# Eight raw weight buffers instead of four in a fused decoder layer with a streamed mixture of experts, and a new order of a few norm, gather and sum steps

## The chip, the cores and the metric

One core of one Trainium2 chip runs the kernel as one launch. The metric is the device time of an execution in microseconds (us), median over runs; lower is better. All data is float32 in HBM. TensorE (PE in the rows) does the matmuls, VectorE is DVE, ScalarE is ACT, GpSimd is POOL, and SP is the queue engine from which nearly all loads are issued, one after the other.

## The reference

One layer over T = 256 tokens of width 1024, batch 1:

```
n  = rmsnorm(x) ;  proj = n @ w_in                  # 1024 x 5136
o_a = gated linear attention(4 heads) ; o_b = differential attention(4 heads)
merged = sigmoid(gate_a) * (o_a @ w_branch_a) + sigmoid(gate_b) * (o_b @ w_branch_b)
h  = x + merged @ w_out
n2 = rmsnorm(h) ;  group = argmax of 4 ; top 2 of the 8 experts in the group
h += sum over 32 experts of comb[e] * ((silu(n2 @ w_gate[e]) * (n2 @ w_up[e])) @ w_down[e])   # 1024 x 256 x 1024 each
h += sigmoid(h @ w_ple_gate) * rmsnorm(p @ w_ple)
out = rmsnorm(h)
```

The expert weights alone are 96 MB, and all of them are read whichever experts the tokens choose.

## The kernel before, in words

**Dense part.** The dense weights are cut into 114 pieces, called units: 8 of `gqk`, 2 of `w_al`, 8 each of `gv`, `dq`, `dk`, `dv` and `gr`, 32 of the gates `sg`, 16 of the branch matrices `y` and 16 of `w_out` (`wo`). A piece is 128x512 float32, 256 KB (the two of `w_al` are smaller). For each piece `raw_load` (L341) takes a buffer with the tag `w_raw` (4 of them) and issues its load on SP; `part` (L347) splits it into a high half, which ACT copies, and a low half, which DVE subtracts (`gv_h` and `gv_l` in the rows, made from `gv_r`); then six matmuls of 512 columns use the two halves: for each of the two token tiles high by high, low by high and high by low. `run` (L383) walks the units in order: it has the loads issued up to unit i+5 and the splitting up to unit i+3. The mixer's own chains (attention, norms, gates) are generators that advance between units.

**Expert weights.** 100 tiles of 1 MB hold the experts' weights and the gate `w_ple_gate`: 8 gate or up tiles and 4 down tiles for each quartet of experts q0 to q7 (`NQ` is 8), and `w_ple_gate` between the down tiles of the last two quartets. They rotate through 23 slots (`ring`, L200); slots 11 to 21 are free from the start, the others hold tensors of the dense part until these die. `NFREE` says how many tiles may be loaded from the start. Every third unit `run` issues one half tile (`refill(whole=False)`) on SP between the raw loads. After the last unit `refill(2 + len(fill))` issues the rest that fits, whole tiles: 23 tiles lie in SBUF before an expert has run, and each later one waits on SP until the matmuls have read the tile that had its slot. SP works in order: a load that waits holds up all that stand behind it.

**Transition.** The last three `w_out` units are held and run by token tile (`out_unit`, L850). `h1_half` (DVE) adds the residual into `xh`; `h1_turn` transposes `xh` on PE (`ph1T`) and copies it out (`h1T`, on ACT, the last on DVE); `h1_square` (ACT) squares `xh` and writes the squares to the spent PSUM bank of `w_out`, which for token tile 0 is the bank that the router's sums `pr` take next. `logits` are the router matmuls `pr`. `inv_root` makes the norm's factor `rstd2`: a DVE addition and a power on POOL with the exponent `mhalf`. `route(t)` is the chain for the top group and the top 2 on DVE, with a small PE matmul `pk` for ranks. `gather(0, t)` multiplies by a one-hot matrix (`pq`) to collect the tokens of the first quartet (`pxg` on PE, evicted into `xg` by DVE); for token tile 0 it yields after its first steps until `pk` of token tile 1 has been issued.

**Experts and end.** `experts_in(q)` runs gate and up (`ph`), then down (`py`), per quartet. In the last quartet the down sums come in quarters (`pyq`, evicted into `ys_last`) and are scattered back to token order by `pz`. Four DVE adds put the output of quartets 0 to 6 and `xh` into `hn`, one 128x512 piece each; `hn` lies in the slot of an expert tile that has been read. Then `pz` is added into `hn`, `hn` is transposed (`ph2T`, copied out as `h2T`), and the gate matmuls `pg` run quarter by quarter. A list of steps (L1383) orders the last gate and norm: `sig`, `mul`, `add`, `square`, `normed` (`sgs = hn * rows`, on POOL or, where V is given, on DVE), `root` (`inv_root` into `ro`), `scaled`, `finished`.

Of the kernel before, what the change touches and what calls it, by code (L numbers as in the profile page):

```python
# [32 lines left out]
NSLOT = 22  # L33
NFREE = NSLOT - 11
ROWS = 8
# [28 lines left out]
def kernel(  # L64
# [38 lines left out]
    def col(t, a):  # L103
        return a[:, t:t + 1]
# [94 lines left out]

    ring = list(range(11, NSLOT)) + [2, 5, 3, 6, 8, 7, 4, 9, 10, 1, 0, NSLOT]  # L200
    ring2 = ring[:15] + ring[19:-1]
# [136 lines left out]
    back, side = lanes = [[], []]  # L338

    def raw_load(i):  # L340
        if i < len(units) and i not in raws and i not in parts and i >= state["i"]:  # L341
            src, kc, n, name = units[i][0]
            raws[i] = wst.tile([P, kc, n], F32, tag="w_raw", name=f"{name}_r", bufs=4)
            Y.dma_start(raws[i], src.rearrange("(k p) n -> p k n", p=P))

    def part(i):
        if i < len(units) and i not in parts:  # L347
            src, kc, n, name = units[i][0]
            if i == 0:
                x_parts(0, [0])  # L350
            elif i < KC:
                x_parts(i)
            if units[i][3]:
                parts[i] = [wst.tile([P, kc, n], F32R, tag=f"w_{c}", name=f"{name}_{c}") for c in "hl"]
                split(parts[i][0], parts[i][1], raws.pop(i), None)
            else:
                parts[i] = raws.pop(i)
            if i == 0:
                x_parts(0, [1])
# [23 lines left out]
    def run(upto):  # L383
        while state["i"] < upto:
            i = state["i"]
            for a in range(5):
                raw_load(i + a)
                if a < 3:
                    part(i + a)
            units[i][1](parts.pop(i))  # L390
            state["i"] = i + 1
            part(i + 3)
            raw_load(i + 5)
            if units[i][2]:
# [428 lines left out]
    for n in range(2):  # L823
        for b, w in enumerate((w_branch_a, w_branch_b)):
            stream([oTs[b][:, i] for i in range(2)], 4, w, n * 512, f"y{b}{n}", branch(b, n), (acc_bank, bank)[n * b])
    accw, held = [], []

    ss2 = cst.tile([P, NT, 2], F32, name="ss2")
# [18 lines left out]
    def h1_square(t, n):  # L847
        A.activation(accw[t][n], xh[:, t, n * 512:(n + 1) * 512], AF.Square, scale=1.0 / 32, accum_out=ss2[:, t, n:n + 1])

    def out_mm(t, n, k, ws):  # L850
        mm3(accw[t][n], [a[:, k, t * P:(t + 1) * P] for a in mT], [w_[:, 0, :] for w_ in ws], k == 0, k == KC - 1)

    def out_unit(k, n):
        def f(ws):
# [17 lines left out]
            h1_half(1, 0)  # L872
            out_mm(1, 1, 6, w61)
            for n_ in range(2):
                h1_turn(0, n_)
            out_mm(1, 1, 7, w71)
            h1_half(1, 1)
            for n_ in range(2):
                h1_square(0, n_)
        return f  # L880

    for k in range(KC):
        for n in range(2):
            units.append(((w_out[k * P:(k + 1) * P, n * 512:(n + 1) * 512], 1, 512, f"wo{n}_{k}"), out_unit(k, n),
                          (lambda: fill.extend(range(2))) if (k, n) == (1, 1) else None, True))

    state["quiet"] = len(units) - 8
    run(len(units))
    while back:
        step()  # L890
    refill(2 + len(fill))
    del fill[:]
# [7 lines left out]
    logits(0, 0)  # L900
    for n in range(2):
        h1_turn(1, n)
    logits(0, 1)
    h1_square(1, 0)
    h1_square(1, 1)
    logits(1, 0)
    logits(1, 1)
# [41 lines left out]
    rk = wk.tile([P, NT, NE], F32, name="rk")  # L949
    rstd2 = wk.tile([P, NT], F32, name="rstd2")  # L950
    mhalf = wk.tile([P, 1], F32, name="mhalf")
    Q.memset(mhalf, -0.5)

    def inv_root(y, ms):

        V.scalar_tensor_tensor(y, ms[0], EPS, ms[1], ALU.add, ALU.add)
        Q.tensor_tensor(y, y, mhalf, ALU.pow)

    for t in range(NT):
        inv_root(col(t, rstd2), (ss2[:, t, 0:1], ss2[:, t, 1:2]))  # L960

# [30 lines left out]
    def route(t):  # L992
# [20 lines left out]
        for i, _ in enumerate(gather(0, t)):  # L1013
            if i:
                yield from until("pk1")
# [124 lines left out]
    def experts_in(q):  # L1140
# [30 lines left out]
        for h in range(2):  # L1171
            last = q == NQ - 1 and h == 1
            E.on = E.on or last
            wts = [wtiles.pop(("gu", q, 4 * h + j)) for j in range(4)]
# [67 lines left out]
    for c in range(LATE):  # L1242
# [3 lines left out]
        wsl[q] = wk.tile([P, 1], F32, name=f"wsl{q}")  # L1246
    last_ys = []

# [18 lines left out]


    first = tiles.index(("gu", NQ - 1, 6))
    hn = slot(slot_of(first - 4), [NT, D], F32, "hn")  # L1270
    for t in range(NT):
        for n in range(2):
            cs = slice(n * 512, (n + 1) * 512)
            V.tensor_tensor(by_rows(hn[:, t, cs]), by_rows(yp[t][n]), by_runs(t, n), ALU.add)
    V.on = A.on = E.on = Q.on = True
# [107 lines left out]
    for f, *a in ((sig, b00), (mul, b00), (sig, b01), (add, b00), (mul, b01), (sig, b10), (square, b00), (normed, 0, 0, 512), (add, b01),  # L1383
                  (mul, b10), (sig, h0), (sig, h1), (normed, 0, 512, 1024), (square, b01), (add, b10), (mul, h0), (square, b10),
                  (add, h0), (root, 0), (mul, h1), (scaled, 0, 0, 512), (square, h0), (add, h1), (scaled, 0, 512, 1024), (square_v, h1),
                  (root, 1), (normed, 1, 0, 512, V), (finished, 1, 512, 768), (scaled, 1, 0, 512, A), (finished, 1, 768, 1024)):
        f(*a)
# [31 lines left out]
```

## Time and profile before

| | |
|---|---|
| median of 3 runs | 448.23 us (448.19 to 448.48) |
| profiled execution | 448.06 us, of which its span is 446.5 us |
| PE busy, DVE busy | 407.3 us (91%), 218.3 us (49%) |
| ACT busy, POOL busy | 154.5 us (35%), 35.7 us (8%) |
| HBM read | 137.62 MB, 311 GB/s over the span |
| mean granted clock of PE | 0.965 |

The profile's page gives whole-span shares; the stages have different limits, so the stretches are read apart: 0 to 201 us the dense units, 201 to 217 us the transition, 217 to 387 us the expert stream, 387 to 436 us the last quartet and the gate, 436 to 446.5 us the last norm. "<-" in brackets names what ended an engine's idle time and how long that was. PE's busy time contains modelled ends of pipelined matmuls, so starts of matmuls are the safer thing to read.

### The profile page before, as it was taken

How to read it: one execution, taken by the hardware profiler on the slowest of the kernel's cores; microseconds unless marked ns; L12 is line 12 of the kernel's file. 1: busy time of each engine (PE TensorE's matmuls, PEld its weight loads, DVE VectorE, ACT ScalarE, POOL GpSimd, SP SyncE). 2: the span in 40 equal slices, each digit the busy share in tenths (PEclk: the TensorE clock that was granted, in tenths of full speed). 3: DMA queues.
4: the chain of work that ended last, by engine and by line, in shares of the span. 5: the costliest groups of instructions: out<-in, count | busy, mean ns of one | idle time of the engine just before them, and what ended most of it. 6: DMA issues, size and time to landing. Idle time of an engine off the chain costs nothing. (4 is left out here: it accounts for less than half of the span.)

```text
span 446.5 us, 7553 instructions
## 1 busy us (share of the span) xinstructions
PE 407.3 (91%) x2876; PEld 273.0 (61%) x2876; DVE 218.3 (49%) x478; ACT 154.5 (35%) x335; POOL 35.7 (8%) x83
## 2 busy tenths in 40 slices
PE   7999999999998999988898988899997998869990
PEld 4767777778786877868545545445263266436670
DVE  4657765896978468656403121222141163073545
ACT  5748645588555535436000000000010100042334
POOL 7200004000160000001000000000000000000003
PEclk9999999999999999999989999989899799988996
DMA  7688875678878888889599999999999999999502
GB/s 222 175 265 277 286 241 156 226 244 283 289 226 275 278 302 274 287 333 349 188 426 418 420 415 420 418 421 419 418 420 420 423 419 420 382 370 364 206 0 94
DMA packets 47214, 139.18 MB, mean 312 GB/s; under 512 B 7282, under 2 KB 17222, under 8 KB 38088
## 3 DMA queue, kind: packets, MB, share of 16 engines
q1 hardware_dynamic: 46872, 138.35, 84.5%
q8 instruction: 23, 0.38, 0.4%
q10 hardware_dynamic: 144, 0.26, 0.2%
q14 instruction: 15, 0.12, 0.1%
q0 software_dynamic: 160, 0.07, 0.1%
HBM read 137.62 MB, written 1.05 MB: 311 GB/s over the span
## 5 line engine op out<-in xcount | busy, mean ns | idle before, releaser
L58 PE MATMUL ph<-wt,xg 128*32 128x256 f32 x1024 | 61.4, 380 | 1.4 <-DMA wt<-in_w_up_dram 1.4
L58 PEld LDWEIGHTS ph<-wt,xg 128*32 128x32 f32 x1024 | 34.4, 110 | 24.5 <-DMA wt<-in_w_up_dram 1.8
L58 ACT ACTIVATE misc<-ph 128x256 f32<-128x256 f32 x8 | 3.1, 384 | 114.6 <-PE ph L58 114.6
L58 PE MATMUL sg<-sg_h,xT 128*128 128x512 f32 x128 | 40.3, 396 | 0.0
L58 PE MATMUL py<-wt,misc 128*32 128x512 f32 x192 | 32.6, 714 | 6.7 <-DVE misc L58 4.7
L58 PEld LDWEIGHTS pxg<-pq,xh 128*128 128x128 f32 x256 | 29.6, 192 | 5.2 <-issue 2.7
L58 PE MATMUL pxg<-pq,xh 128*128 128x128 f32 x256 | 30.4, 276 | 1.9 <-PEq L1061 1.6
L58 DVE TENSOR_TENSOR sg_l<-sg_r,sg_h 128x512 fp32r<-128x512 f32 x32 | 23.5, 736 | 10.5 <-ACT sg_h L58 10.4
L58 PE MATMUL pg<-wg,h2T 128*128 128x512 f32 x96 | 27.2, 420 | 0.7 <-ACT h2T L58 0.7
L58 PEld LDWEIGHTS sg<-sg_h,xT 128*128 128x128 f32 x128 | 23.4, 188 | 4.3
L58 PE MATMUL sg<-sg_l,xT 128*128 128x512 f32 x64 | 25.3, 395 | 0.1
L58 ACT ACTIVATE sg_h<-sg_r 128x512 fp32r<-128x512 f32 x32 | 19.9, 628 | 14.6 <-DMA sg_r<-in_w_in_dram 8.9
L58 PEld LDWEIGHTS py<-wt,misc 128*32 128x32 f32 x192 | 7.4, 124 | 26.8 <-issue 16.0
L58 DVE TENSOR_TENSOR xg<-pxg,g_exp 128x512 f32<-128x512 f32 x16 | 11.0, 690 | 23.0 <-PE pxg L58 22.7
L58 DVE SCALAR_TENSOR_TENSOR misc<-df,wr 128x128 f32<-128x128 bf16 x16 | 3.9, 288 | 37.1 <-PE phT L58 37.0
L58 PEld LDWEIGHTS pg<-wg,h2T 128*128 128x128 f32 x96 | 17.5, 198 | 7.2 <-issue 2.9
L58 PE MATMUL wo<-wo_h,mT 128*128 128x512 f32 x64 | 20.2, 396 | 1.3 <-ACT wo_h L58 1.3
L58 POOL TENSOR_TENSOR sgs<-hn,rows 128x512 f32<-128x512 f32 x2 | 2.5, 1282 | 229.3 <-DVE hn L58 229.3
L58 PE MATMUL y<-y_h,oT 128*128 128x512 f32 x64 | 20.1, 395 | 0.0
L58 DVE TENSOR_TENSOR wo_l<-wo_r,wo_h 128x512 fp32r<-128x512 f32 x16 | 11.0, 691 | 10.2 <-ACT wo_h L58 9.8
L58 DVE TENSOR_TENSOR y_l<-y_r,y_h 128x512 fp32r<-128x512 f32 x16 | 10.9, 691 | 8.3 <-ACT y_h L58 8.3
L58 PE MATMUL y<-late,misc 128*128 128x512 f32 x32 | 14.9, 608 | 0.0
(312 smaller groups left out, 738.7 us busy)
## 6 DMA issues: line engine op xcount, KB each, us to landing
wt<-in_w_up_dram SPq DMA_DIRECT2D x27, 1024.0 KB, 19.2
wt<-in_w_gate_dram SPq DMA_DIRECT2D x24, 1024.0 KB, 19.8
wt<-in_w_down_dram SPq DMA_DIRECT2D x20, 1024.0 KB, 19.8
wt<-in_w_down_dram SPq DMA_DIRECT2D x24, 512.0 KB, 9.3
wt<-in_w_gate_dram SPq DMA_DIRECT2D x16, 512.0 KB, 5.2
sg_r<-in_w_in_dram SPq DMA_DIRECT2D x32, 256.0 KB, 3.2
wt<-in_w_up_dram SPq DMA_DIRECT2D x10, 512.0 KB, 4.5
wo_r<-in_w_out_dram SPq DMA_DIRECT2D x16, 256.0 KB, 4.7
```

What stands on the lines that cost most here:

```text
L58: ins = getattr(self.engine, name)(*args, **kwargs)
```

## The change

1. Raw weight pieces have eight buffers: four with the tag `w_raw`, four in `more`, which is slot 20 of the experts' slots; groups of four units alternate. Loads are issued up to unit i+8 instead of i+5. The two halves of the very last unit go into two `w_raw` buffers.
2. `NFREE` is 10 instead of 11 and `ring` is reordered: slot 20 gets its first tile only at the transition, where three whole tiles more than `len(fill)` are issued instead of two. During the units 16 tiles are loaded instead of 17.
3. `h1_square(0, 0)` is issued ahead of the two transposes of token tile 0. `rstd2` and its exponent lie in the dead tiles `sinT` and `cosT`, and `rstd2` of a token tile is computed as soon as its squares are, between the transposes.
4. Token tile 0's gather goes on to its third step before it waits for `pk` of token tile 1.
5. The four adds into `hn` are issued (`own_order`) ahead of the last half of the last quartet's gate and up matmuls.
6. In the final list `normed(1, 0, 512)` moves from DVE to POOL and up, `root 0` ahead of `add h0`, and `scaled 0` behind `add h1`.

```diff
-NFREE = NSLOT - 11
+NFREE = NSLOT - 12
...
-    ring = list(range(11, NSLOT)) + [2, 5, 3, 6, 8, 7, 4, 9, 10, 1, 0, NSLOT]
+    ring = list(range(11, NSLOT - 2)) + [NSLOT - 1, 2, 5, 3, 6, 8, 7, 4, 9, 10, NSLOT - 2, 1, 0, NSLOT]
...
+    more = slot(NSLOT - 2, [4, 512], F32, "more_r")
...
-            raws[i] = wst.tile([P, kc, n], F32, tag="w_raw", name=f"{name}_r", bufs=4)
+
+            raws[i] = wst.tile([P, kc, n], F32, tag="w_raw", name=f"{name}_r", bufs=4) if (i + 2) // 4 % 2 else \
+                more[:, (i + 2) % 4, :].rearrange("p (k n) -> p k n", k=kc)
...
-                parts[i] = [wst.tile([P, kc, n], F32R, tag=f"w_{c}", name=f"{name}_{c}") for c in "hl"]
+                tag, bufs = ("w_raw",) * 2 if i == state.get("last") else ("w_h", "w_l"), 4 if i == state.get("last") else None
+                parts[i] = [wst.tile([P, kc, n], F32R, tag=tag[c], name=f"{name}_{'hl'[c]}", bufs=bufs) for c in range(2)]
...
-            for a in range(5):
+            for a in range(8):
...
-            raw_load(i + 5)
+            raw_load(i + 8)
...
+    rstd2, mhalf = sinT[:, 0, 0:2], cosT[:, 0, 0:1]
+    Q.memset(mhalf, -0.5)
...
+            h1_square(0, 0)
             for n_ in range(2):
                 h1_turn(0, n_)
             out_mm(1, 1, 7, w71)
             h1_half(1, 1)
-            for n_ in range(2):
-                h1_square(0, n_)
+            h1_square(0, 1)
...
-    refill(2 + len(fill))
+    refill(3 + len(fill))
...
     logits(0, 0)
-    for n in range(2):
-        h1_turn(1, n)
+    h1_turn(1, 0)
+    norm2(0)
+    h1_turn(1, 1)
     logits(0, 1)
     h1_square(1, 0)
     h1_square(1, 1)
+    norm2(1)
...
-            if i:
+            if i > 2:
                 yield from until("pk1")
...
+            if last:
+                own_order()
...
+    def own_order():
+
+        hn_.append(slot(slot_of(first - 4), [NT, D], F32, "hn"))
+        for t in range(NT):
+            for n in range(2):
+                cs = slice(n * 512, (n + 1) * 512)
+                V.tensor_tensor(by_rows(hn_[0][:, t, cs]), by_rows(yp[t][n]), by_runs(t, n), ALU.add)
...
-                  (add, h0), (root, 0), (mul, h1), (scaled, 0, 0, 512), (square, h0), (add, h1), (scaled, 0, 512, 1024), (square_v, h1),
-                  (root, 1), (normed, 1, 0, 512, V), (finished, 1, 512, 768), (scaled, 1, 0, 512, A), (finished, 1, 768, 1024)):
+                  (normed, 1, 0, 512), (root, 0), (add, h0), (mul, h1), (square, h0), (add, h1), (scaled, 0, 0, 512), (square_v, h1),
+                  (root, 1), (scaled, 0, 512, 1024), (finished, 1, 512, 768), (scaled, 1, 0, 512, A), (finished, 1, 768, 1024)):
```

The first place is SP around the last raw loads of `w_out`; `wo_5_r` is the raw piece of `w_out`'s row block 5, `wt` an expert tile (128x2048 is a whole one, 128x1024 a half), and the two fences are the kernel before and the changed one.

```order
L58 DMA wo_4_r<-in_w_out_dram 128x512
L58 DMA wo_5_r<-in_w_out_dram 128x512 x2
L58 DMA wt_2054<-in_w_up_dram 128x1024
L58 DMA wo_6_r<-in_w_out_dram 128x512 x2
L58 DMA wo_7_r<-in_w_out_dram 128x512 x2
L58 DMA wt_2054<-in_w_up_dram 128x1024
L58 DMA wt_2162<-in_w_up_dram 128x2048
```

```order
L58 DMA wo_4_r<-in_w_out_dram 128x512 x2
L58 DMA wo_5_r<-in_w_out_dram 128x512 x2
L58 DMA wt_1962<-in_w_gate_dram 128x1024
L58 DMA more_r<-in_w_out_dram 128x512 x3
L58 DMA wt_1962<-in_w_gate_dram 128x1024
L58 DMA more_r<-in_w_out_dram 128x512
L58 DMA wt_2104<-in_w_up_dram 128x2048
```

The last four raw pieces are loaded into `more`, and they are issued up to eight units ahead of their matmuls instead of five; behind the last of them no half tile is left, and whole tiles follow at once.

The second place is ACT in the transition, where `wo_0` and `wo_1` are the spent `w_out` banks that take the squares of token tiles 0 and 1, and `h1T` the copies of the transposes.

```order
L58 ACTIVATE wo_7_h<-wo_7_r 128x512 x2
L58 ACTIVATE h1T_2147<-ph1T_2142 128x512
L58 ACTIVATE h1T_2154<-ph1T_2149 128x512
L58 ACTIVATE wo_0_1947,ss_1659<-xh 128x512
L58 ACTIVATE wo_0_1948,ss_1659<-xh 128x512
L58 ACTIVATE h1T_2184<-ph1T_2179 128x512
```

```order
L58 ACTIVATE wo_7_h<-more_r 128x512 x2
L58 ACTIVATE wo_0_1901,ss_1619<-xh 128x512
L58 ACTIVATE h1T_2090<-ph1T_2085 128x512
L58 ACTIVATE h1T_2097<-ph1T_2092 128x512
L58 ACTIVATE wo_0_1902,ss_1619<-xh 128x512
L58 ACTIVATE h1T_2127<-ph1T_2122 128x512
```

One square has moved from behind the two copies to ahead of them; the other stays behind.

The third place is DVE in the last quartet: `misc` is the quartet's gated product, `ys_last` the evicted down sums, `hn` the sum that the last gate reads.

```order
L58 CAST oT_last<-pws_3540 128x256
L58 SCALAR_TENSOR_TENSOR misc<-misc,wsl_3378,ph_3548 128x256
L58 TENSOR_TENSOR ys_last<-pyq_3622,ys_last 128x256
L58 COPY misc<-phT_3619 128x256
L58 TENSOR_TENSOR hn<-y_2435,xh 128x512
L58 TENSOR_TENSOR hn<-y_2436,xh 128x512
L58 TENSOR_TENSOR hn<-y_2437,xh 128x512
L58 TENSOR_TENSOR hn<-y_2438,xh 128x512
L58 TENSOR_TENSOR ys_last<-pyq_3650,ys_last 128x256
```

```order
L58 CAST oT_last<-pws_3480 128x256
L58 TENSOR_TENSOR hn<-y_2375,xh 128x512
L58 TENSOR_TENSOR hn<-y_2376,xh 128x512
L58 TENSOR_TENSOR hn<-y_2377,xh 128x512
L58 TENSOR_TENSOR hn<-y_2378,xh 128x512
L58 SCALAR_TENSOR_TENSOR misc<-misc,wsl_3318,ph_3488 128x256
L58 TENSOR_TENSOR ys_last<-pyq_3567,ys_last 128x256
L58 COPY misc<-phT_3564 128x256
L58 TENSOR_TENSOR ys_last<-pyq_3590,ys_last 128x256
```

The four adds stand ahead of the gated product instead of between the two evictions of the down sums.

## Rows read from the trace of the kernel before

**Rows 1.** A piece of the chain of waits: start, length, what.

```profile
367.12 19.95 DMA wt<-in_w_up_dram
```

**Rows 2.** SP's issues at the transition, by the timeline; the fourth of them waits for the first slot that the experts free.

```profile
200.89 16.40 SPq L58 DMA_DIRECT2D wt<-in_w_down_dram  x4
```

**Rows 3.** Windows: the stretch and its length, then busy time and count of PE, PEld, DVE, ACT and POOL, then granted clock of PE, DMA share, GB/s.

```profile
211.50:217.00 5.50, 5.50 (x88) 3.92 (x90) 3.18 (x10) 0.43 (x1) 0.00 (x0) 1.00 0.08 31
220.00:387.00 167.00, 150.51 (x1406) 79.94 (x1398) 41.00 (x105) 9.03 (x21) 0.00 (x0) 0.95 1.01 419
398.30:405.00 6.70, 5.83 (x26) 3.23 (x27) 3.50 (x5) 0.98 (x2) 0.00 (x0) 0.51 1.07 372
405.00:420.00 15.00, 15.00 (x108) 10.46 (x108) 5.90 (x9) 5.54 (x8) 0.00 (x0) 0.99 1.00 343
```

**Rows 4.** Timeline of SP (issues) and PE while the `gv` units run: start, length, engine, operation, and the idle time before it with what ended it.

```profile
15.86 5.96 SPq L58 DMA_DIRECT2D gv_r<-in_w_in_dram  x4
25.68 0.73 PE L58 MATMUL gv<-gv_h,xT 128*128 128x512 f32 x2 [0.44 <-ACT gv_h L58]
33.71 0.73 PE L58 MATMUL gv<-gv_h,xT 128*128 128x512 f32 x2 [0.59 <-ACT gv_h L58]
34.69 0.50 PE L58 MATMUL gv<-gv_l,xT 128*128 128x512 f32 x1 [0.24 <-DVE gv_l L58]
```

**Rows 5.** One row of PE's waits over the first 200 us: who waited for whom, us in total, times, longest.

```profile
PE poT L58 <- DVE osl L58: 1.6, 2, 0.8
```

**Rows 6.** Timeline of SP, ACT and PE at the end of `w_out`, columns as in rows 4.

```profile
186.46 3.81 SPq L58 DMA_DIRECT2D wo_r<-in_w_out_dram  x4
195.96 0.63 ACT L58 ACTIVATE wo_h<-wo_r 128x512 fp32r<-128x512 f32 x1 [2.56 <-DMA wo_r<-in_w_out_dram]
194.52 0.62 PE L58 MATMUL wo<-wo_h,mT 128*128 128x512 f32 x2
194.98 0.40 PE L58 MATMUL wo<-wo_l,mT 128*128 128x512 f32 x1
196.64 0.73 PE L58 MATMUL wo<-wo_h,mT 128*128 128x512 f32 x2 [1.26 <-ACT wo_h L58]
199.31 1.09 PE L58 MATMUL ph1T<-ident,xh 128*128 128x128 f32 x8
200.16 0.70 PE L58 MATMUL wo<-wo_h,mT 128*128 128x512 f32 x2
200.70 0.40 PE L58 MATMUL wo<-wo_l,mT 128*128 128x512 f32 x1
```

**Rows 7.** Timeline of ACT and PE at the first router sums.

```profile
200.97 0.61 ACT L58 ACTIVATE wo<-xh 128x512 f32<-128x512 f32 x1
201.80 1.05 PE L58 MATMUL pr<-wr,h1T 128*128 128x40 f32 x8 [0.70 <-issue]
```

**Rows 8.** Timeline of PE in the gather for the first quartet.

```profile
209.96 0.18 PE L58 MATMUL pk<-Mb,scr 128*128 128x32 bf16 x1 [0.32 <-DVE Mb L58]
209.99 3.37 PE L58 MATMUL pxg<-pq,xh 128*128 128x128 f32 x28
```

**Rows 9.** Timeline of ACT, DVE and PE after the last expert tile has landed.

```profile
394.24 0.38 ACT L58 ACTIVATE ys_last<-pyq 128x256 fp32r<-128x256 f32 x1 [0.69 <-PE pyq L58]
392.74 3.95 DVE L58 TENSOR_TENSOR hn<-y,xh 128x512 f32<-128x512 f32 x4
396.60 0.42 DVE L58 TENSOR_TENSOR ys_last<-pyq,ys_last 128x256 fp32r<-128x256 f32 x1
397.08 0.62 PE L58 MATMUL pz<-ys_last,oT_last 128*128 128x256 f32 x3 [2.02 <-DVE ys_last L58]
398.48 1.12 PE L58 MATMUL ph2T<-ident,hn 128*128 128x128 f32 x4 [0.79 <-DVE hn L58]
400.28 1.65 PE L58 MATMUL pg<-wg,h2T 128*128 128x512 f32 x3 [0.69 <-ACT h2T L58]
401.86 1.94 PE L58 MATMUL pyq<-wt,misc 128*32 128x256 f32 x16
406.70 1.07 PE L58 MATMUL pyq<-wt,misc 128*32 128x256 f32 x16
410.60 0.60 PE L58 MATMUL ph2T<-ident,hn 128*128 128x128 f32 x4
412.78 1.07 PE L58 MATMUL pyq<-wt,misc 128*32 128x256 f32 x16
416.08 1.07 PE L58 MATMUL pyq<-wt,misc 128*32 128x256 f32 x16
```

**Rows 10.** Timeline of DVE and POOL at two places where both work in SBUF: the first two rows in the dense part, the others at the end.

```profile
135.44 0.69 DVE L58 TENSOR_TENSOR rs_a<-ro 128x8 f32<-128x8 f32 x1
135.28 0.83 POOL L58 TENSOR_TENSOR wr<-wr,g_exp 128x320 f32<-128x320 f32 x1 [4.97 <-DMA wr<-in_w_router_expert_dram]
435.40 2.55 POOL L58 TENSOR_TENSOR sgs<-hn,rows 128x512 f32<-128x512 f32 x2 [229.34 <-DVE hn L58]
438.87 0.55 POOL L58 TENSOR_TENSOR ro<-ro,mhalf 128x1 f32<-128x1 f32 x1 [0.93 <-DVE ro L58]
440.88 0.69 DVE L58 TENSOR_TENSOR sgs<-hn,rows 128x512 f32<-128x512 f32 x1
441.04 0.93 POOL L58 TENSOR_TENSOR ro<-ro,mhalf 128x1 f32<-128x1 f32 x1 [1.62 <-DVE ro L58]
```

More of the change, by code (lines that the diff above doesn't have):

```diff
@@ L826, with inv_root, norm2 @@
     accw, held = [], []
+    rstd2, mhalf = sinT[:, 0, 0:2], cosT[:, 0, 0:1]
+    Q.memset(mhalf, -0.5)
+    def inv_root(y, ms):
+        V.scalar_tensor_tensor(y, ms[0], EPS, ms[1], ALU.add, ALU.add)
+        Q.tensor_tensor(y, y, mhalf, ALU.pow)
+    def norm2(t):
+        inv_root(col(t, rstd2), (ss2[:, t, 0:1], ss2[:, t, 1:2]))
     ss2 = cst.tile([P, NT, 2], F32, name="ss2")
@@ L885 @@
                           (lambda: fill.extend(range(2))) if (k, n) == (1, 1) else None, True))
+    state["last"] = len(units) - 1
     state["quiet"] = len(units) - 8
@@ L949 @@
     rk = wk.tile([P, NT, NE], F32, name="rk")
[L950 to L960, printed above, removed]
     def sm(shape, name, dt=F32):
@@ L1246 @@
         wsl[q] = wk.tile([P, 1], F32, name=f"wsl{q}")
-    last_ys = []
+    last_ys, hn_ = [], []
+    first = tiles.index(("gu", NQ - 1, 6))
+    def own_order():
[4 more added lines that the diff above has]
+                V.tensor_tensor(by_rows(hn_[0][:, t, cs]), by_rows(yp[t][n]), by_runs(t, n), ALU.add)
     def outs_of(c, i):
@@ L1265 @@
         experts_in(q)
[L1269 to L1274, printed above, removed]
+    hn = hn_[0]
     V.on = A.on = E.on = Q.on = True
```

## The prediction, made before the changed kernel ran

> **What bounds the kernel now.** I read the chain of waits first, then windows by stage, then the timelines at the seams. The chain's piece that ends last before the tail is the load of an expert tile, 367.12 + 19.95 = 387.07 [rows 1]. The windows say why: from 220 to 387 the DMA share is 1.01 at 419 GB/s, while PE has 16 us of the 167 to spare [rows 3]. So there the time is bytes over rate, and nothing that engines gain inside the stretch shortens it. What counts is when the stream may start. SP's fourth issue in the group that begins at 200.89 goes out at the group's end, 200.89 + 16.40 less its own third of a microsecond, at 217.0: a tile has to wait for the first slot that an expert's matmuls free [rows 2]. Ahead of it the DMA engines stand nearly idle, share 0.08 from 211.5 to 217 [rows 3], since the 23 tiles that fit are already in. The kernel therefore falls into three parts in series: PE work and chains of latencies up to the first freed slot; a stream of fixed length, 387.1 - 217.0 = 170 us; a tail of PE, DVE and ACT behind the last tile. A microsecond taken from the first or the third comes off the total; one taken from the second by an engine does not.
>
> **The change part by part.** *A tile's load moved from the units into the transition.* 23 tiles are in before the first slot comes free in both kernels; only 16 instead of 17 of them load during the units. The tile moved costs 1 MB at 419 GB/s, 2.5 us of DMA, against 5.5 us in which DMA idles at 0.08 [rows 3]. I cost it at nothing; if that cover were gone it would be at most 2.5.
>
> *Eight buffers, early.* While `gv` runs, SP takes 5.96 us to issue four raw loads, which wait for buffers [rows 4]. Each wait becomes a late piece: PE stands 0.44 + 0.59 + 0.24 = 1.27 us for `gv` halves [rows 4]. With loads issued eight units ahead the pieces are in when they are wanted; I take 1.3. PE's other waits of these 200 us are for the mixers' own chains, the largest 1.6 us for `osl` [rows 5]; they hang on DVE, not on loads, and might go if DVE is held less by late halves. Bounds: 0.5 if only one `gv` wait goes, 2.9 if the 1.6 goes too.
>
> *Eight buffers, end of `w_out`.* The four last raw loads take SP 3.81 us from 186.46, the last issue thus at about 190.0; its piece ends ACT's wait of 2.56 at 195.96, and PE stands 1.26 from there [rows 6]. Worked on PE's clock of starts: two columns-of-512 matmuls are 194.98 - 194.52 = 0.46 apart, 0.23 each, so PE is free at 195.21. From there come 12 more such matmuls (2.76) and the 8 transposes (200.16 - 199.31 = 0.85): 198.8 without waits. Before, the last one ends its turn at 200.70 + 0.23 = 200.93. That is 2.1 us: the 1.26, the refilling of the pipeline behind it, and the short wait of the transposes for `xh`, whose first sum stood on DVE behind the late low half. In the changed order the last four pieces are issued three units earlier, 18 x 0.23 = 4.1 us, which exceeds ACT's 2.56, so I take 2.1; lower bound the bare 1.3.
>
> *Squares and `rstd2`.* The router sums `pr` start at 201.80 after 0.70 that no engine released [rows 7]. They take the bank in which ACT's first square runs from 200.97 to 201.58 [rows 7]: they waited for their bank. With that square ahead of the copies the bank is free when the sums come. I take 0.65 of the 0.70, lower bound 0.2 if the copies of the transposes come later by the square's 0.61 instead. The earlier `rstd2` of token tile 0 moves a step that is not last: the next DVE step waits for the squares of tile 1 in either order. Nothing for it.
>
> *Gather.* PE stands 0.32 us until it may do the rank matmul `pk` at 209.96, with 28 gather matmuls behind it, 3.37 us or 0.12 each [rows 8]. Four more of them (the two program instructions that are moved count as four in the trace) now lie ahead of it and fill most of the gap. I take 0.3; bounds 0 and 0.45. The transition gives 2.1 + 0.65 + 0.3, 3.05 in all.
>
> *The four adds.* They occupy DVE from 392.74 for 3.95 us, and the eviction that needs only ACT's `ys_last` of 394.24 + 0.38 = 394.62 starts behind them at 396.60 [rows 9]. PE's `pz` waits 2.02 for it. Ahead of the last half of the quartet DVE has nothing to do until the product at 391, so the adds are covered there, provided their inputs and the slot for `hn` are free by 391.2 - 3.95 = 387.3. Gain 396.60 - 394.66 = 1.9; bounds 0 and 1.94.
>
> *The clock in the tail.* The granted clock is 0.51 from 398.3 to 405 and 0.99 from 405 on, half speed and full speed (1.2 and 2.4 GHz); what stands ahead of the fall is PE's gap of 2.02 us before `pz` and the short work behind it [rows 3, 9]. The price is read from equal work at both levels. Between two groups of `pyq`: 406.70 - 401.86 = 4.84 at half speed, 416.08 - 412.78 = 3.30 at full. That is 1.54; the three `pg` before take 401.86 - 400.28 = 1.58, where three at 0.23 are 0.69, and some of the rest is the filling of the pipeline, say 0.66 of slowness. 2.2 together; with the four transposes, 1.12 against 0.60, 2.7 [rows 9]. Once the adds are out, the gap before `pz` is some 0.1 us instead of 2.02, and only waits under a microsecond are left (0.79 and 0.69). I hold it likelier than not that the clock stays up: 2.2, bounds 0 and 2.7.
>
> *The final list.* `root 0`, whose DVE addition has two inputs in SBUF, moves ahead of `add h0`, while POOL now runs a third `normed` of 2.55 / 2 = 1.28 us from about 437.95 [rows 10]. Two places show what such pairs do. The 128x8 product `rs_a` took 0.69 and ended at 136.13, where the POOL product beside it ended at 136.11; the small power took 0.93 beside DVE's `sgs` and 0.55 alone [rows 10]. So the addition, ready at about 438.3, would be held until 439.2 and the adds behind it some 0.5 later at `root 1`; in return the second power no longer meets DVE's `sgs` and gives back 0.93 - 0.55 = 0.38. I take 0 for the whole list; bounds a loss of 0.2 and, without the hold, a gain of 0.84 (0.46 from the shorter queue on DVE, 0.38).
>
> The Trainium skill, SBUF — State Buffer, section "Who interferes with whom", states that a DVE instruction with two SBUF inputs contends with a GpSimd one that reads SBUF, and that the later of the two blocks fully. It speaks against this edit, and both pairs of rows 10 agree with it; by the opposite view, no lock, the list would be worth the 0.84 and the sum would end near 438.9.
>
> **The sum.** 1.3 + 3.05 + 1.9 + 2.2 + 0 = 8.45, say 8.5, off the profiled execution's 448.06: 439.6. The median stands 0.17 above that execution, so 439.7.
>
> **The rivals.**
>
> *A, the clock falls all the same.* The waits of 0.79 and 0.69 before `ph2T` and `pg` remain, and with them PE is still half idle for a stretch [rows 9]; within the expert stream, where PE idles 16 us in pieces, the mean is 0.95 [rows 3], so there the clock does fall at times. Then 2.2 stays: 441.9. Chance 0.34.
>
> *B, the adds are not covered.* If `hn`'s slot is released late, by the last half's own matmuls, DVE waits at the adds with the product behind them, which PE needs. The gain of 1.9 goes and the clock's 2.2 with it: 443.8, and more by what the slot is later than 391.2. It decides from a release after 387.3. For it speaks that the slot is that of one of the last tiles; against it that this tile stands four ahead of the last two, among matmuls that were over before the wait for the 387.07 landing. Chance 0.07.
>
> *C, the buffers do nothing.* The change would not do what it says if the late pieces came from sharing DMA bandwidth with the half tiles and not from their issue. Then `gv` still waits (1.3) and so does `w_out` (2.1): 443.1. For it, DMA takes five microseconds from issue to landing here (190 to 195.96); against it, that time is the same when issued earlier. Chance 0.07.
>
> *D, slower: SP stuck behind a half tile.* With one slot fewer, each tile from the eleventh on goes to a slot that it reaches earlier in the order than before, and slots of dense tensors come free only as these die. A half tile whose slot is still read holds all raw loads behind it. Eight pieces in hand cover 8 x 6 x 0.23 = 11 us. Half tiles come every third unit, 4.1 us, so a slot one tile late, two points, is 8.3 us and hidden; the bound decides at three points. A slot held for six, 24.8 us, would cost PE 13.8: 439.7 + 13.8 = 453.5. SP's raw issues show waits of about a microsecond each now [rows 4, 6], nothing near that. Chance 0.03.
>
> **How the numbers follow.** Forecast 0.49, A 0.34, B 0.07, C 0.07, D 0.03. The likeliest is 439.7. Its own bounds, taken together, are 436.4 (early 2.9, transition 3.2, adds 1.9, clock 2.7, list 0.84) and some 442. The range for 8 in 10 takes in A with its small misses and the near edge of B and C: 436.4 to 443.5. A measurement of this kernel can tell about 0.2%, 0.9 us. All cases but D are faster by far more than that; I leave 0.01 for gains that are lost piece by piece. Faster 0.96, same 0.01, slower 0.03.
>
> **What would show it.** Right: no PE wait for `gv`; no wait for `wo_h` at the last unit; `pr` starting without 0.7 of nothing; the first freed slot at about 217.0 - 4.4 = 212.6 and the last tile's landing at 382.7, their distance still 170; the four adds over before the product, with DVE idle behind them; `pz` without its 2.02; granted clock 1.00 behind it. A is told by 0.5 in the 7 us after `pz`. B by DVE idle ahead of the adds until after the last landing. C by the same PE waits with raw loads issued earlier. D by one long wait of SP on a half tile. The prediction is wrong in its base if the distance from first freed slot to last landing grows, for then the seven whole tiles or a slot's new place has pushed the stream; or in the tail, if a matmul waits for a load there: the tail's loads still run at 343 GB/s up to 420 [rows 3], and a tail shorter by 4.1 comes that much nearer to them.

## The result and the profile after

The changed kernel took 436.66 us (median of 4 runs, 435.37 to 440.63) beside 448.21 before: ratio 0.9748, interval 0.9707 to 0.9789. In a second series it took 435.54 (435.19 to 435.62), ratio 0.9691, interval 0.9663 to 0.9719. The forecast was 439.7 in a range of 436.4 to 443.5: right in direction and, for the first series, inside the range near its low end; the second lies 0.9 below it. There are two profiles of the changed kernel, one of 440.63 and one of 435.51 us, and the 5 us between them are a finding of their own. One execution of `depth5` took 1013.29 us where its five others took 433.87 to 436.63, and its figures below are those of the five.

Both, and every experiment below, are read by one table. Its cuts are the start of the last `wo_h` matmuls, the first `ph` of the first quartet, the `ph` behind the last expert tile, and the end of the span (us).

| profile | dense units | transition | expert stream | tail |
|---|---|---|---|---|
| before | 200.5 | 12.8 | 173.8 | 59.4 |
| changed, first | 196.4 | 12.5 | 173.9 | 56.2 |
| changed, second (`after_again`) | 192.8 | 12.5 | 173.8 | 54.8 |
| `bufs_alone` | 193.8 | 16.0 | 174.0 | 59.4 |
| `bufs_place` | 192.5 | 16.0 | 174.0 | 59.4 |
| `bufs_norm` | 193.9 | 13.2 | 173.9 | 59.0 |
| `trans_alone` | 200.2 | 12.2 | 173.9 | 59.4 |
| `adds_alone` | 203.0 | 12.8 | 174.0 | 54.7 |
| `lambda_first` | 209.2 | 12.5 | 173.9 | 56.2 |
| `end_dve` | 193.6 | 12.5 | 174.0 | 54.2 |
| `lambda_actq` | 192.8 | 12.5 | 173.9 | 56.3 |
| `depth5` | 192.2 | 12.5 | 173.8 | 56.3 |
| `warm_tail` | 193.3 | 12.5 | 173.9 | 54.7 |
| `best` | 192.9 | 12.5 | 173.9 | 54.2 |

The stream is 174 us in all fourteen: what the first freed slot gains, the end gains, as the base of the prediction had it. The gain from before to the second profile is 7.7 + 0.3 + 0 + 4.6 = 12.6. The dense units differ from profile to profile with the same loads and buffers: 200.2 to 203.0 in the three with four buffers (mean 201.2), 192.2 to 196.4 in the ten with eight, `lambda_first` left out (mean 193.4). So a difference of two or three us in this column is not one that single profiles can show; the 7.7 is, and the means give 7.8.

The stage of dense units, by one row for each of four tiles' matmuls: count, ns of one (least, median, most), first and last start. Before:

```profile
L58 PE MATMUL gv<-gv_h,xT x32: 387/393/577, 22.2 to 36.6; 128*128 128x512 f32 x32
L58 PE MATMUL sg<-sg_h,xT x128: 387/389/481, 98.1 to 149.8; 128*128 128x512 f32 x128
L58 PE MATMUL y<-y_h,oT x64: 387/389/496, 150.2 to 174.4; 128*128 128x512 f32 x64
L58 PE MATMUL wo<-wo_h,mT x64: 387/389/497, 174.9 to 200.5; 128*128 128x512 f32 x64
```

and the second profile of the changed kernel:

```profile
L58 PE MATMUL gv<-gv_h,xT x32: 387/389/580, 22.2 to 34.2; 128*128 128x512 f32 x32
L58 PE MATMUL sg<-sg_h,xT x128: 387/389/481, 97.1 to 146.4; 128*128 128x512 f32 x128
L58 PE MATMUL y<-y_h,oT x64: 387/389/481, 146.8 to 169.1; 128*128 128x512 f32 x64
L58 PE MATMUL wo<-wo_h,mT x64: 387/389/481, 169.6 to 192.8; 128*128 128x512 f32 x64
```

`gv` is shorter by 2.4, `sg` by 2.4, `y` by 1.9 and `w_out` by 2.4; `dq`, between them, is longer by 1.4. (By first and last start, the ten profiles with eight buffers lie at least 1.7 under the three with four in each of the four stages, so these gains are clear of the spread.) PE's idle rows had shown 1.27 for `gv` [rows 4], 1.6 for `osl` [rows 5], which lies inside `sg` (137 to 141 us), and 1.26 for `w_out` [rows 6]; `y` has one of 0.69 (`pmT`, at 166.82) that the prediction does not list. The waits of the weight loads (PEld), which the prediction did not read, show more of it; three of their rows for the first 200 us of before:

```profile
PEld gv L58 <- ACT gv_h L58: 2.3, 3, 1.0
PEld gv L58 <- DVE gv_l L58: 1.5, 3, 0.7
PEld wo L58 <- ACT wo_h L58: 1.7, 1, 1.7
```

and one for the second profile of the changed kernel, where no row for `wo` or `y` is left:

```profile
PEld gv L58 <- DVE gv_l L58: 0.6, 1, 0.6
```

The first profile shows where its dense units lost 3.7 us to the second. Timeline of DVE and PE:

```profile
42.21 0.29 DVE L58 TENSOR_TENSOR tmp<-tmp 128x128 f32<-128x128 f32 x1 [4.56 <-DMA tmp<-in_lambda_k_dram]
43.48 0.50 PE L58 MATMUL dq<-dq_l,xT 128*128 128x512 f32 x1 [1.40 <-DVE dq_l L58]
45.96 1.20 PE L58 MATMUL dq<-dq_h,xT 128*128 128x512 f32 x2
```

DVE, in order, stands 4.56 us for a load of 64 numbers (32 KB, as it goes to all 128 partitions) that a product needs; the low halves `dq_l` wait behind it, PE waits 1.40, and then two matmuls take 1.20 instead of 0.62 at a granted clock of 0.66 from 44 to 48 us. The same profile also has slow first units: up to about 11 us their matmuls start 0.43 apart, not 0.23 (0.63 for one at 8.39 us), and `gv` starts 1.1 later. That is the pace of half clock, but the windows call the clock 1.00 there: the trace's first record of a granted clock comes only at 11.1 us (5.0 in the second profile), so half clock is likely and not shown.

The end of `w_out` and the router in the first profile (timeline of PE and DVE, to be read against [rows 6 to 8]):

```profile
195.08 0.39 PE L58 MATMUL wo<-wo_l,mT 128*128 128x512 f32 x1
195.31 1.06 PE L58 MATMUL ph1T<-ident,xh 128*128 128x128 f32 x8
196.68 0.39 PE L58 MATMUL wo<-wo_l,mT 128*128 128x512 f32 x1
196.90 0.98 PE L58 MATMUL pr<-wr,h1T 128*128 128x40 f32 x8
198.19 1.09 PE L58 MATMUL ph1T<-ident,xh 128*128 128x128 f32 x8 [0.31 <-DVE xh L58]
203.62 0.18 PE L58 MATMUL pk<-Mb,scr 128*128 128x32 bf16 x1 [0.55 <-DVE r_g L58]
205.88 3.14 PE L58 MATMUL pxg<-pq,xh 128*128 128x128 f32 x24
```

No wait for `wo_h` and none ahead of `pr`: both went as forecast. But behind `pr` the transposes of token tile 1 now wait 0.31 for their residual sum. The first freed slot is SP's fourth issue here; first and second profile, against 217.0 [rows 2]:

```profile
196.87 16.07 SPq L58 DMA_DIRECT2D wt<-in_w_down_dram  x4
```

```profile
193.17 16.07 SPq L58 DMA_DIRECT2D wt<-in_w_down_dram  x4
```

that is about 212.6 and 208.9. The tail of the first profile, timeline and windows (columns as in [rows 3]):

```profile
376.25 3.88 DVE L58 TENSOR_TENSOR hn<-y,xh 128x512 f32<-128x512 f32 x4 [2.82 <-PE ph L58]
390.42 1.08 PE L58 MATMUL pz<-ys_last,oT_last 128*128 128x256 f32 x4
392.28 0.66 PE L58 MATMUL ph2T<-ident,hn 128*128 128x128 f32 x4 [0.78 <-DVE hn L58]
393.63 1.65 PE L58 MATMUL pg<-wg,h2T 128*128 128x512 f32 x3 [0.69 <-ACT h2T L58]
395.20 1.86 PE L58 MATMUL pyq<-wt,misc 128*32 128x256 f32 x16
399.29 1.07 PE L58 MATMUL pyq<-wt,misc 128*32 128x256 f32 x16
```

```profile
391.00:392.30 1.30, 0.52 (x4) 0.31 (x4) 0.76 (x2) 1.18 (x2) 0.00 (x0) 1.00 1.10 351
393.60:395.00 1.40, 1.37 (x3) 0.83 (x3) 1.39 (x2) 0.00 (x0) 0.00 (x0) 0.50 1.08 364
395.00:397.00 2.00, 2.00 (x18) 0.60 (x17) 0.43 (x1) 0.00 (x0) 0.00 (x0) 0.54 1.05 386
397.00:399.00 2.00, 2.00 (x15) 1.70 (x11) 0.42 (x1) 0.39 (x1) 0.00 (x0) 1.00 1.07 375
```

The adds are covered and `pz` has lost its 2.02 us [rows 9]. The clock still fell, but for some 3.4 us instead of 6.7. In the second profile it did not:

```profile
388.50:392.00 3.50, 2.74 (x24) 1.50 (x25) 2.97 (x4) 0.90 (x3) 0.00 (x0) 1.00 1.09 365
392.00:399.00 7.00, 7.00 (x48) 5.23 (x49) 2.67 (x4) 2.94 (x5) 0.00 (x0) 1.00 1.07 363
```

And the final list in the first profile, DVE and POOL, against [rows 10]:

```profile
430.75 1.11 DVE L58 SCALAR_TENSOR_TENSOR ro<-sso,sso 128x1 f32<-128x1 f32 x1
427.98 3.87 POOL L58 TENSOR_TENSOR sgs<-hn,rows 128x512 f32<-128x512 f32 x3 [224.84 <-DVE hn L58]
433.94 0.55 POOL L58 TENSOR_TENSOR ro<-ro,cosT 128x1 f32<-128x1 f32 x1 [1.45 <-DVE ro L58]
```

`root 0`'s addition ends at 431.86, POOL's third product at 431.85: held, as forecast. The second power takes 0.55 instead of 0.93. From the last transposes to the end it is 17.1 us here and before.

### The profile page after: what moved, and what is told of

It is laid out like the page before. It is cut to its first block, busy times and chain, and to the rows that moved or that the text cites. A ratio compares the mean times of both kernels' runs of the same rounds, so it can differ in the third digit from the quotient of the medians.

```text
span 439.0 us, 7555 instructions
## 1 busy us (share of the span) xinstructions
PE 402.5 (92%) x2876; PEld 276.8 (63%) x2876; DVE 218.9 (50%) x477; ACT 155.7 (35%) x335; POOL 37.2 (8%) x84
## 4 chain that ended last, share of the span: by engine, by line
PE 56%; DMA 37%; DVE 3%; issue 1%; ACT 1%; SPq 0%; POOL 0%; POOLq 0%; DVEq 0%
DMA wt<-in_w_up_dram 14%; DMA wt<-in_w_down_dram 12%; PE sg L58 10%; DMA wt<-in_w_gate_dram 8%; PE y L58 6%; PE pg L58 6%; PE wo L58 5%; PE ph L58 3%; PE gqk L58 3%; PE dv L58 3%; PE dk L58 3%; PE gr L58 3%; PE pyq L58 2%; PE pxg L58 2%; PE dq L58 2%; DMA tmp<-in_lambda_k_dram 2%
## 5 line engine op out<-in xcount | busy, mean ns | idle before, releaser
L58 PE MATMUL ph<-wt,xg 128*32 128x256 f32 x1024 | 62.3, 380 | 3.4 <-DMA wt<-in_w_up_dram 3.4
L58 PEld LDWEIGHTS ph<-wt,xg 128*32 128x32 f32 x1024 | 35.3, 110 | 26.5 <-DMA wt<-in_w_up_dram 4.9
L58 PE MATMUL py<-wt,misc 128*32 128x512 f32 x192 | 30.0, 674 | 7.6 <-DVE misc L58 4.7
L58 PEld LDWEIGHTS pxg<-pq,xh 128*128 128x128 f32 x256 | 29.7, 192 | 4.9 <-issue 2.3
L58 PEld LDWEIGHTS py<-wt,misc 128*32 128x32 f32 x192 | 7.1, 120 | 26.0 <-issue 14.3
L58 POOL TENSOR_TENSOR sgs<-hn,rows 128x512 f32<-128x512 f32 x3 | 3.8, 1275 | 224.9 <-DVE hn L58 224.8
L58 DVE TENSOR_TENSOR xg<-pxg,g_exp 128x512 f32<-128x512 f32 x16 | 11.1, 691 | 23.2 <-PE pxg L58 22.9
L58 DVE TENSOR_TENSOR sg_l<-sg_r,sg_h 128x512 fp32r<-128x512 f32 x16 | 12.6, 789 | 3.7 <-ACT sg_h L58 3.6
L58 DVE TENSOR_TENSOR sg_l<-more_r,sg_h 128x512 fp32r<-128x512 f32 x16 | 11.8, 746 | 4.6 <-ACT sg_h L58 4.5
L58 PEld LDWEIGHTS sg<-sg_l,xT 128*128 128x128 f32 x64 | 12.0, 188 | 2.6
L58 PEld LDWEIGHTS y<-y_h,oT 128*128 128x128 f32 x64 | 11.9, 188 | 2.4
```

What stands on the lines that cost most here:

```text
L58: ins = getattr(self.engine, name)(*args, **kwargs)
```

## The experiments

The kernel before varied between 446.5 and 452.0 in these series, so that ratios have intervals of about 0.4%; in the transition and the tail the table above, not the medians, tells parts of a microsecond or two apart.

**One part alone, on the kernel before.** `bufs_alone`: the first two points of the change (buffers, depth, last halves, ring).

```diff
-            raw_load(i + 5)
+            raw_load(i + 8)
...
+    more = slot(NSLOT - 2, [4, 512], F32, "more_r")
```

> Only the eight raw buffers, the deeper loads, the last unit's halves and the slots that go with them. Theory (late pieces cost more than the idle rows say, and the small loads on the same queue are the price): the first expert matmul comes 4 us earlier when DVE is held at the product of the lambda loads and 8 us earlier when it is not, so 440 to 444.5, with a spread of several us between runs that the kernel before does not have. Rival, the prediction's sizes: 1.3 + 2.1 = 3.4 less, 444.8, spread as before. Rival C of the prediction: under 1 us.

443.61 (442.57 to 446.19), ratio 0.9886 (0.9854 to 0.9918). The dense units gain 6.7 us, twice the prediction's 3.4. But the transition is 3.2 longer than before, so that in this profile only half of it arrives; the medians of the series differ by 5.4. Timeline of POOL, DVE and PE there:

```profile
199.75 0.10 POOL L58 MEMSET one<- 128x1 f32 x1 [0.64 <-PE pr L58]
200.23 1.10 POOL L58 TENSOR_TENSOR rstd<-rstd,mhalf 128x1 f32<-128x1 f32 x2
200.84 0.26 DVE L58 SCALAR_TENSOR_TENSOR lg<-pr,rstd,brt 128x40 f32<-128x40 f32 x1 [1.70 <-POOL rstd L58]
203.20 0.18 PE L58 MATMUL pk<-Mb,scr 128*128 128x32 bf16 x1 [2.31 <-DVE r_g L58]
205.49 4.41 PE L58 MATMUL pxg<-pq,xh 128*128 128x128 f32 x28
```

and the first constant and the first `pk` in the kernel before:

```profile
199.33 0.10 POOL L58 MEMSET one<- 128x1 f32 x1
207.74 0.18 PE L58 MATMUL pk<-Mb,scr 128*128 128x32 bf16 x1 [0.19 <-DVE r_g L58]
```

On POOL the constants `onesb`, `one`, `scr` stand ahead of the two powers, and `one` waits until PE has done with `pr`. Before, it ran with no such wait, 2.5 us ahead of the first `pr` [rows 7]. So this is a wait that the buffers' edit brings, and not one that was hidden: all eleven profiles with eight buffers have it, none of the three with four. Why is not shown; that the constants come to lie in memory that `pr` still reads is the likely reason. PE, idle for 2.3 us, then gathers at a granted clock of 0.50 from 205 to 207 us (28 matmuls in 4.41 us; 3.37 before [rows 8]).

`adds_alone`: only the four adds moved.

```diff
+            if last:
+                own_order()
```

> Only the four adds into hn moved ahead of the last half quartet. Theory from the changed kernel's profile: 1.9 for the eviction and 1.2 of 2.2 for the clock, which still falls but later and for a shorter time: 445.1. Prediction's sizes: 1.9 + 2.2 = 4.1, 444.1. Rival A (clock as before): 446.3.

445.69 (444.22 to 448.84), ratio 0.9928 (0.9902 to 0.9955). The tail is 54.7 against 59.4: 1.95 for the eviction and 2.7 for the clock, which stayed at 1.00 in this profile:

```profile
399.00:405.00 6.00, 5.03 (x38) 3.18 (x42) 3.62 (x5) 1.37 (x3) 0.00 (x0) 1.00 1.07 372
```

From the first `ph2T` to the last group of them it is 30.9 us before, 29.7 in the changed kernel's first profile, 28.2 in its second and 28.1 here. That gives the clock's term two sizes, 1.2 and about 2.7, by whether it falls again.

`trans_alone`: the square, `rstd2` and the gather.

```diff
+            h1_square(0, 0)
             for n_ in range(2):
                 h1_turn(0, n_)
...
+    norm2(0)
     h1_turn(1, 1)
...
-            if i:
+            if i > 2:
```

> Only the transition's order: square, rstd2, gather. Theory: the router sums come 0.7 earlier but the second token tile's transposes then wait for its residual sum on DVE, so only 0.3 to 0.4 is left: 447.8. Prediction's sizes: 0.65 + 0.3, 447.3.

447.83 (445.69 to 450.49), ratio 0.9979 (0.9954 to 1.0004): no difference that the runs can tell, and 0.6 in its transition, where the prediction had 0.95 and nothing of it for `rstd2`. The next two show that with the buffers `rstd2`'s part is worth more than the other two together.

**With the buffers, which part of `rstd2`'s edit counts.** `bufs_norm` adds to `bufs_alone` the place and the early issue of `rstd2`, without the square's and the gather's moves; `bufs_place` adds the place alone:

```diff
-    rstd2 = wk.tile([P, NT], F32, name="rstd2")
-    mhalf = wk.tile([P, 1], F32, name="mhalf")
+    rstd2, mhalf = sinT[:, 0, 0:2], cosT[:, 0, 0:1]
```

> Eight buffers and, of the transition's order, only the place and the early issue of rstd2 (powers on POOL ahead of the constants). Theory: with the buffers alone the powers stood on POOL behind constants whose memory PE was still reading, and the router's first step waited 1.7 us for them; now it does not, PE's wait of 2.3 us before the first rank matmul falls under 0.6, and 2.1 to 3.5 us come off the buffers' own time (443.6), 440 to 441.5. Rival (rstd2's edit is worth nothing, as the prediction had it): 443.6.

> Eight buffers, and rstd2 and its exponent put into the dead tiles, but issued where they stood before, behind the constants on POOL. Theory (order on POOL decides): as the buffers alone, 443.6, with the router's first step still waiting for POOL. Rival (the memory of rstd2 itself decides): as with the early issue, 440 to 441.5.

`bufs_norm` 440.94 (439.89 to 441.61), ratio 0.9805 (0.9767 to 0.9843), transition 13.2; `bufs_place` 443.10 (442.24 to 443.57), ratio 0.9855 (0.9817 to 0.9893), transition 16.0. The router's first step in `bufs_place`, then POOL's first power and PE's first `pk` in `bufs_norm`:

```profile
199.54 0.26 DVE L58 SCALAR_TENSOR_TENSOR lg<-pr,sinT,brt 128x40 f32<-128x40 f32 x1 [2.08 <-POOL sinT L58]
```

```profile
196.11 0.58 POOL L58 TENSOR_TENSOR sinT<-sinT,cosT 128x1 f32<-128x1 f32 x1 [63.65 <-DVE sinT L58]
201.56 0.18 PE L58 MATMUL pk<-Mb,scr 128*128 128x32 bf16 x1 [0.55 <-DVE r_g L58]
```

The order decides and the place does nothing: 2.9 us of transition, 1.0 of it the gather that no longer runs at half clock at first.

**The lambda load.** `lambda_first` issues the four small loads from ACT at the start and takes them out of the list of small loads:

```diff
+    for j, l in enumerate((lambda_q1, lambda_k1, lambda_q2, lambda_k2)):
+        A.dma_start(lams[:, j, :], l.to_broadcast([P, 64]))
```

> The changed kernel with the four small lambda loads issued from ACT's queue at the start instead of from SP between the raw loads. Theory (DVE stands 4.6 us for the last of them, behind eight raw loads in the same queue, PE then 1.9 us and the clock falls): no wait of DVE for a lambda load, no PE wait in dq, and the spread of the changed kernel (435.4 to 440.6) shrinks to its low end, 434.8 to 436. Rival (the spread is the clock's or the memory's own): still 435 to 441.

451.72 (450.69 to 453.42), ratio 1.0063 (1.0041 to 1.0086): a miss, and it tells nothing of the question. Four steps taken out of one generator moved all the mixers' steps behind it forward; PE then waited 3.3 us for the `diff_subln` load and 3.1 for POOL, and the dense units took 209.2. `lambda_actq` keeps the steps and changes the queue alone:

```diff
-            Y.dma_start(dst, src)
+            (A if dst.shape[-1] == 64 else Y).dma_start(dst, src)
```

> The changed kernel with only the queue of the four lambda loads changed, SP to ACT, at the same points of the program. Theory (the last lambda load lies behind the deeper raw loads in SP's queue): DVE's wait for it, 3.4 and 4.6 us in two profiles of the changed kernel, falls under 1 us, PE has no wait for dq_l, and the stage of dq takes 14.6 to 15 us instead of 16.0 and 18.6; 434.3 to 435.5 with a spread under 1 us. Rival (the wait is for the core's DMA engines, whichever queue): DVE still waits 3 us or more, 435.5.

436.09 (435.54 to 440.79), ratio 0.9734 (0.9684 to 0.9783). Issued at 33.30 from ACT, and still

```profile
39.52 0.29 DVE L58 TENSOR_TENSOR tmp<-tmp 128x128 f32<-128x128 f32 x1 [3.61 <-DMA tmp<-in_lambda_k_dram]
```

It landed at 39.40, 6.1 us after its issue. So my theory of the queue fell: the load is as slow from ACT's queue. That it waits for the DMA engines is then the likely reason, not a shown one. `depth5` has eight buffers and the old depth:

```diff
-            raw_load(i + 8)
+            raw_load(i + 5)
```

> The changed kernel with its eight buffers, but loads issued only up to unit i+5 as before. Theory (what counts is that a load is issued before its buffer's wait, so that depth in time matters and not the number of buffers): issue at i+5 with free buffers still gives 5 x 1.36 = 6.8 us for a load of 3 to 6 us, so nearly all of the gain stays, and DVE's wait for the lambda load shrinks: 435 to 437. Rival (the depth itself is the gain): gv, sg, y and wo take again what they took before, 440 to 442.

434.80 (433.87 to 436.63), ratio 0.9688 (0.9643 to 0.9734). The whole gain of the dense units stays (192.2, though this profile's first units were slow like the first one's), and the wait is gone; SP and DVE:

```profile
29.96 0.43 SPq L58 DMA_DIRECT2D tmp<-in_lambda_k_dram  x1
36.93 0.29 DVE L58 TENSOR_TENSOR tmp<-tmp 128x128 f32<-128x128 f32 x1
```

With as many loads ahead as buffers, SP stands in its order at the load that waits for the splitting of unit i, and all that is written behind it, the lambda loads too, goes out late (the last of them at 35.20 and 34.32 in the two profiles of the changed kernel, 29.96 here). With three fewer ahead the same loads find free buffers. It is the number of buffers that gains. The depth gains nothing that these runs show and costs in `dq`: 14.3 us from first to last start here, 15.1 to 18.4 in the nine profiles with the depth of eight. The times do not tell 434.80 from 435.54, as the intervals of their ratios overlap.

Beside the kernel before, though, the loads are not late. Its SP and DVE, and DVE in the second profile of the changed kernel:

```profile
36.34 0.43 SPq L58 DMA_DIRECT2D tmp<-in_lambda_k_dram  x1
40.27 0.29 DVE L58 TENSOR_TENSOR tmp<-tmp 128x128 f32<-128x128 f32 x1 [0.48 <-DMA dq_r<-in_w_in_dram]
```

```profile
40.01 0.29 DVE L58 TENSOR_TENSOR tmp<-tmp 128x128 f32<-128x128 f32 x1 [3.45 <-DMA more_r<-in_w_in_dram]
```

Before, the last load went out at 36.34, later than in the changed kernel, and DVE waited 0.48. With eight buffers DVE comes to the product 2.1 and 3.2 us earlier, and from issue to product it takes 7.0 and 5.7 us instead of 3.9. (The profile names a raw load that ended about then as what the product waited for; the load that it needs is the lambda load beside it.)

**The end and the clock.** `after_again` is the changed kernel a second time, with no edit.

> The changed kernel itself once more, for a second profile and its spread beside the others. Theory: the tail is 56.1 us from the last tile's matmuls to the end of the span if the clock falls for a short time after the adds, and 54.6 if it does not; the first freed slot lies near 213 if DVE's wait for the lambda load reaches PE, and near 209 if it does not. Times 435 to 441. Rival: the spread comes from the expert stream, whose 170 us would then differ between the two profiles.

435.54 (435.19 to 435.62). It gave the second profile: tail and dense units account for all of the difference, and the stream is the same 173.8.

`end_dve` gives the last `normed` back to DVE:

```diff
-(normed, 1, 0, 512), (root, 0), (add, h0)
+(root, 0), (add, h0)
...
-(root, 1), (scaled, 0, 512, 1024)
+(root, 1), (normed, 1, 0, 512, V), (scaled, 0, 512, 1024)
```

> The changed kernel with the last normed back on DVE at its old place; root 0 stays ahead of add h0. Theory (root 0's addition is held 1.0 us by POOL's third normed): the addition takes 0.15 instead of 1.11, the second power takes 0.9 instead of 0.55, and the stretch from the last h2T transposes to the end shrinks by 0.5, from 17.1 to 16.6. Rival (no hold, the 1.11 is something else): the addition stays near 1.1 and the stretch grows by 0.4.

436.81 (434.89 to 439.85), ratio 0.9732 (0.9692 to 0.9771). The median does not tell it from the changed kernel, the rows do:

```profile
426.56 0.15 DVE L58 SCALAR_TENSOR_TENSOR ro<-sso,sso 128x1 f32<-128x1 f32 x1
428.85 0.94 POOL L58 TENSOR_TENSOR ro<-ro,cosT 128x1 f32<-128x1 f32 x1 [1.52 <-DVE ro L58]
```

The hold is gone, the power meets DVE's product again, and the last stretch is 16.6 instead of 17.1, as expected: moving `normed` to POOL gives away the 0.5 that the rest of the new list gains.

`warm_tail` fills PE's two short waits of the tail with dummy transposes.

```diff
     scatter(1, 0)
+    keep_warm(3)
     turn(0)
+    keep_warm(3)
```

> The changed kernel with three dummy transposes of the identity in each of PE's two short waits around the first h2T transposes. Theory (the clock falls in some runs because PE is half idle there): granted clock 1.00 all through the tail in every profile, tail 54.8 us plus at most 0.3. Rival (the fall comes from elsewhere): a profile with half clock behind them, tail 56 us or more.

435.82 (434.76 to 436.70), ratio 0.9706 (0.9667 to 0.9745), tail 54.7, granted clock 1.00 from 388 to 395:

```profile
388.00:395.00 7.00, 6.87 (x57) 4.81 (x59) 4.07 (x5) 2.15 (x4) 0.00 (x0) 1.00 1.08 369
```

`best` joins it with `lambda_actq` and `end_dve`.

> The changed kernel with the lambda loads on ACT's queue, the dummy transposes and the last normed back on DVE. Sum of the parts against 435.5: lambda 0.7 to 1.4, normed 0.5, clock 0 where it did not fall: 433.6 to 434.5. Rival (the dq stage's gain is lost again at the transition): 435.

435.40 (434.82 to 436.60), ratio 0.9708 (0.9669 to 0.9746), with the shortest tail, 54.2, and the clock up. The lambda part gave nothing, so it misses its forecast. In seven profiles with early adds and no dummies the clock fell in four (tails of 56.2 to 56.3) and not in three; with dummies it fell in neither of two. That fits, but two profiles don't show it. Eight buffers at the depth of five together with these two edits of the tail was not tried.

## Why the prediction came out as it did

The forecast gain was 8.5, the measured one 11.55 in the first series. The number fell in the range with some luck. The larger sizes that the prediction lists add up to 11.54, which leaves 436.7 off the median of 448.23, and not 436.4, and the measured 436.66 lies just there. In the first profile the first freed slot came at 212.6, the very number forecast, because 3.7 us lost to slow matmuls and the lambda load took back half of a gain of 7.7 that had been put at 3.4. Part by part:

*Early buffers: mis-sized.* The term was 1.3 with bounds 0.5 and 2.9. Measured in the second profile: `gv` 2.4, `sg` 2.4 and `y` 1.9, less 1.4 that `dq` lost, 5.3 net. The step that failed is the reading of PE's idle rows as the price of late pieces. Ends of matmuls are modelled, so a wait shorter than the modelled overlap shows no idle time. [rows 4] have an example: of the two `gv_h` matmuls at 33.71 and the `gv_l` at 34.69 the starts are 0.98 apart where two paces of 0.23 are 0.46, which is 0.52 lost with 0.24 shown as idle. The first-to-last starts of a stage, and PEld's waits (3.8 for `gv` where PE's rows gave 1.27), bracket it. The second part of the failure is "they hang on DVE, not on loads": the waits for `osl` fell from 1.6 to nothing in both profiles of the changed kernel and to 0.4 and 0.5 in `bufs_alone` and `depth5`. That DVE was no longer held by late halves is the likely reason; no run tests it alone.

*End of `w_out`: right.* 2.1 forecast, 2.4 for the whole stage measured. There the prediction counted matmul starts instead of idle rows.

*Transition: wrong in its parts.* 0.95 forecast; 0.3 in the table, which is the sum of three: the buffers lengthen the transition by 3.2 (`bufs_alone`), the early powers take back 2.9 (`bufs_norm`), the square and the gather 0.7 (the changed kernel against `bufs_norm`). The gather gave 0.2 of its 0.3. The square brought `pr` 0.9 forward, but 0.4 of that went again, because the transposes of token tile 1 then waited for `xh`. The step "Nothing for it" on `rstd2` failed: in the kernel before the powers did stand where they cost nothing, but with the buffers POOL's constants ahead of them got a new wait for `pr`. A price read in the kernel before does not hold for an edit once another edit has changed what stands in front of it.

*The adds: right.* 1.9 forecast, 1.95 by the position of `ph2T` behind the last tile (11.37 before, 9.42 after). Rival B was wrong: the adds ran from 376.25, long before the product.

*The clock: right or between it and rival A, by the run.* 2.2 forecast; 1.2 in the first profile, 2.7 in the second, where rival A had 0. The price was nearer its upper bound of 2.7; whether it is paid the prediction could not know.

*The final list: right.* 0 forecast, 0.0 measured (17.1 us before and after), with the hold and the 0.38 both as worked out. `end_dve` confirms the reason. The Trainium skill (SBUF — State Buffer, "Who interferes with whom") states that the ports that DVE and GpSimd share are an exclusive lock and that the later of two such instructions blocks fully. The trace agrees: 1.11 us beside POOL's product, 0.15 without it.

*Stream and moved tile: right.* 174 us throughout; no wait of SP over 0.1 us ahead of a half tile (rival D). Rival C fell with the dense units' 6.7.

*What was not foreseen:* the lambda load. DVE comes to the product earlier, the load lands about when it did before or later, and DVE's order carries the wait to PE: 1.40 us in the first profile, with a fall of the clock behind it, and about 0.2 in the second. The three extra loads ahead keep the small loads from going out sooner, as `depth5` shows.

## What to carry to other kernels

Price a late operand by the first-to-last starts of the stage against count times pitch, with the weight loads' waits as a check; the idle rows of a pipelined engine were a lower bound here. When two edits meet on one path, cost the second in the order, and the memory, that the first leaves behind: an operation with slack now may be the next wait. More buffers and a deeper queue are two edits; take the buffers, and look at what stands behind the deeper loads in the issuing engine's order.

## What the runs showed of the hardware

A load of 32 KB issued from ACT's queue was as slow as from SP's (6.1 us from issue to landing; 5.7 and 7.0 from issue to DVE's product in the changed kernel, 3.9 before): the queue that issues a load made no difference here. DVE's 1-column addition took 1.11 us beside a POOL product and 0.15 without it, and ended within 0.01 us of that product. Equal code ran with the granted clock at 1.00 or near 0.5 in the same stretch of different runs, at `dq` (0.66 from 44 to 48 us in the first profile, 1.00 in the second) and in the tail (0.50 and 1.00), where it is worth 1.5 us. The first units' slow pace, in some runs alone, cost 1.1 us.
